# Step sizes' projection with both weight parts in one block of 128 columns, norms with shorter chains, one load per head

## The chip, the cores and the metric

The kernel runs on one core of one Trainium2 chip. The metric is device time in microseconds (us) of one execution, median of several. Engines are named as in the profile: PE (TensorE, matrix products), ACT (ScalarE), DVE (VectorE), POOL (GpSimd), SP (SyncE, which here only issues DMAs).

## What is computed

A trunk of two layers on 512 tokens of width 1024, all float32. Each layer is a token mixer and a GeGLU channel mixer, each between two RMS norms. The first mixer is retention and neighbourhood attention, the second a bidirectional state-space mixer (SSD). Cut to what the change touches:

```
def rms_norm(x, g):
    y = x * rsqrt(mean(x * x, axis=-1) + EPS)
    return y * g

def ssd_mixer(hn, w_in, ...):
    z, xbc, dt_raw = split(hn @ w_in)                # dt_raw: 64 step sizes per token
    dt = softplus(dt_raw + dt_bias)
    log_a = dt * -exp(a_log)                         # summed over the tokens of a chunk
    y = bidir_scan(q, k, x * dt_f, x * dt_b, log_a)  # per head: exp of differences of sums
    y = (y + x * d_skip) * silu(z)
    y = y * rsqrt(mean(y * y, over each of 4 groups) + EPS) * norm_g
    return y @ w_out

for layer in range(2):
    x = x + rms_norm(mixer(rms_norm(x, g0)), g1)
    x = x + rms_norm(ffn(rms_norm(x, g2)), g3)
```

## The kernel before

The 512 tokens are four tiles (t = 0 to 3) of 128 rows. Activations stand transposed on chip, features on partitions, as `xh` and `xl`: a float32 value is split into a rounded part (`hi`, written by an ACT copy) and the rest (`lo`, written by a DVE subtraction); `split`, L80 to L83, does that. Weights arrive as `wst` and are split in the same way into `whi` and `wlo`. A product is then three matmuls (`mm3`, L85 to L89): hi with hi, lo with hi, hi with lo; the product of both rests is left out.

Norms. `norm` squares a row tile on ACT with a running sum (`sumsq`, output thrown into a scratch tile `junk` of the ring `tmp`), DVE adds epsilon (`v_x`), POOL raises to the power -0.5 (`r_x`), and DVE scales into `xs` (L132). `turn` transposes `xs` on PE (`pt`, L141) and splits it into `xh`, `xl`. Behind a mixer, `post_half` squares each half row (`ssm0`, `ssm1`) and multiplies it by the gain (`mg`, L151); `post_norm` then adds the two sums (`v_m`, L110), POOL makes `r_m`, and DVE adds into `x` (L176).

The second mixer, `mixer1`, works through four groups of eight heads. `steps` projects the 64 step sizes (L589 to L598), makes softplus, prefix sums and their exponentials, and leaves them in two DRAM scratch tensors, `pd` (sums) and `yd` (decays), in `etot` (decay of a whole chunk, spread over the partitions by a matmul into `pe`, L635) and in `tok` (per-token factors: `lp_e`, whose logarithm is taken at L650, and `sw`, both transposed at L655). `load` brings one head's rows of `pd`, spread over 128 partitions, as `pb`; `head` adds `tok` (eight ACT pieces, L754), selects, and takes `e` (L758). `inter` and `pair` make the outputs `pi` and `py` of two heads each, `rms` the group norm (`pss`, one-column matmuls of squares with `mean`, then POOL's power `rg`). Weights of the next projections are used in between as fillers.

What sets the order: each group's list of slots (`SLOTS`) gives the program order, and a scheduler places every instruction on its engine's queue by its own estimates; engines run their queues strictly in that order. Tiles come from rings of fixed size, so a write also waits for the last reader of the memory it takes over. DMAs are issued by SP, those of `pb` by ACT.

The end of `mixer1` (the loop over `TAIL`) runs the output projection of the last group tile by tile, with the norms of the finished tiles between; the first matmuls of the channel mixer follow as soon as `xh` and `xl` of two tiles stand.

Of the kernel before, what the change touches and what calls it, by code (L numbers as in the profile page):

```python
# [10 lines left out]
U32 = mybir.dt.uint32  # L11
# [15 lines left out]
class Env:  # L27


    def __init__(self, ctx, tc):  # L30
# [11 lines left out]
        pool("pad", 1).tile([P, 32], F32, name="pad")  # L42
# [9 lines left out]
        self.x = self.res.tile([P, NT, D], F32, name="x")  # L52
# [53 lines left out]
    def inv_rms(self, name, a, b=None):  # L106
# [3 lines left out]
        nc.vector.tensor_scalar(v, a, EPS, b, op0=ALU.add, **({"op1": ALU.add} if b is not None else {}))  # L110
# [4 lines left out]
    def sumsq(self, src, n, name):  # L115

        s = self.small.tile([P, 1], F32, name=name)
        w = src.shape[-1]
        junk = self.tmp.tile([P, w], BF16, name="junk", tag="tmp")
        self.nc.scalar.activation(junk, src, AF.Square, scale=float(n) ** -0.5, accum_out=s)  # L120
# [14 lines left out]
    def turn(self, t):  # L135

        nc = self.nc
        for h, xs in enumerate(self.xs[t]):
# [15 lines left out]
    def finish(self, steps, st, done):  # L154
        for step in steps.split():
# [5 lines left out]
            elif t in self.xs:  # L161
                self.turn(t)
# [136 lines left out]
def mixer0(E, w0, w_v, w_fm, tabs, dist_d, logit, gn, bias, w_out, g_post_row, done):  # L299
# [254 lines left out]
def mixer1(E, w_dt, w_fm, cw, dtc, cols, mask, w_out, g_post_row, done):  # L554
# [7 lines left out]
    with ExitStack() as ctx:  # L562
# [25 lines left out]
        def steps():  # L588
# [479 lines left out]
```

## Time and profile before

| what | value |
|---|---|
| median of 3 runs | 1425.6 us (1424.62 to 1425.9) |
| the profiled execution | 1426.99 us |
| its span in the trace | 1425.2 us (1.8 us lie around it) |
| PE busy | 1398.7 us, 98% |
| DVE, ACT, POOL busy | 909.0, 706.9, 61.1 us |

PE has 26 us of idle time in all; whatever moves the time must remove PE work, remove such idle time, or change the clock at which PE runs. The trace gives PE's granted clock as a share of 2.4 GHz: 1.00, or 0.50, which is 1.2 GHz. Starts and lengths below are in us from the start of the span; a matmul's row shows its own latency, and matmuls of 512 columns follow each other at about 0.23 us.

### The profile page before, as it was taken

What the parts mean: (1) busy time and instruction counts of PE and PEld (TensorE: products, weight loads), DVE (VectorE), ACT (ScalarE), POOL (GpSimd) and SP (SyncE); (2) the same over time, 40 slices, a digit from 0 to 9 for tenths busy, and PEclk for the clock granted to TensorE, in tenths of its full rate; (3) what the DMA queues carried; (4) which work ended last, traced back from release to release, by engine and by line L of the source; (5) the groups of instructions that cost most, each with busy time, mean ns of one, the idle gap of its engine ahead of it and who ended that gap; (6) DMA issues with size and microseconds to landing.
All of it is one profiled execution on the core that took longest, in us unless ns stands there. A gap on an engine that the chain in (4) does not pass through costs nothing.

```text
span 1425.2 us, 17860 instructions
## 1 busy us (share of the span) xinstructions
PE 1398.7 (98%) x6838; PEld 1143.5 (80%) x6838; DVE 909.0 (64%) x1359; ACT 706.9 (50%) x1192; POOL 61.1 (4%) x66
## 2 busy tenths in 40 slices
PE   7999999999999999999999999999989999999998
PEld 6877776898888888888778788787878888888886
DVE  7378888666565652447788786897785665664232
ACT  5346666444444431334777888585354444443230
POOL 0010110100000000000000110000110000000000
PEclk9999999999999999999999999999999999999999
DMA  8443232233323223323556454463342233233231
GB/s 286 150 133 99 85 97 76 84 101 97 100 92 104 89 89 113 111 109 108 141 172 192 134 189 148 135 167 98 114 151 74 90 103 91 101 97 96 89 104 59
DMA packets 56949, 166.34 MB, mean 117 GB/s; under 512 B 7200, under 2 KB 7968, under 8 KB 56864
## 3 DMA queue, kind: packets, MB, share of 16 engines
q1 hardware_dynamic: 47648, 148.42, 32.4%
q10 hardware_dynamic: 9216, 16.78, 4.4%
q8 instruction: 54, 0.88, 0.2%
q14 instruction: 31, 0.25, 0.1%
HBM read 157.57 MB, written 5.51 MB: 114 GB/s over the span
## 4 chain that ended last, share of the span: by engine, by line
PE 91%; ACT 3%; DVE 3%; issue 1%; DMA 1%; POOL 0%; DVEq 0%; SPq 0%; POOLq 0%; ACTq 0%
PE mm L87 27%; PE mm L88 27%; PE mm L89 27%; PE pi L775 2%; PE st L723 1%; PE py L795 1%; PE y L450 1%; PE pt L141 1%; PE pt L667 1%; PE sc L434 1%; PE sc L435 0%; DMA x<-in_x 0%; PE pt L502 0%; PE y L512 0%; PE sc L485 0%
## 5 line engine op out<-in xcount | busy, mean ns | idle before, releaser
L87 PE MATMUL mm<-xh,whi 128*128 128x512 f32 (+1 forms) x1216 | 465.1, 383 | 2.5 <-ACT z L693 2.0
L89 PE MATMUL mm<-xl,whi 128*128 128x512 f32 (+2 forms) x1216 | 464.4, 382 | 3.0 <-DVE xl L83 3.0
L88 PE MATMUL mm<-xh,wlo 128*128 128x512 f32 (+2 forms) x1216 | 463.5, 381 | 0.0
L83 DVE TENSOR_TENSOR wlo<-wst,whi 128x1024 fp32r<-128x1024 f32 (+1 forms) x208 | 254.9, 1226 | 132.3 <-ACT whi L82 130.5
L82 ACT CAST whi<-wst 128x1024 fp32r<-128x1024 f32 (+1 forms) x208 | 216.6, 1043 | 151.4 <-PE mm L88 109.2
L87 PEld LDWEIGHTS mm<-xh,whi 128*128 128x128 f32 x1216 | 229.2, 188 | 48.3 <-issue 2.7
L89 PEld LDWEIGHTS mm<-xl,whi 128*128 128x128 f32 (+1 forms) x1216 | 229.1, 189 | 47.5 <-DVE xl L83 3.2
L88 PEld LDWEIGHTS mm<-xh,wlo 128*128 128x128 f32 (+1 forms) x1216 | 229.3, 189 | 42.5 <-issue 0.4
L228 DVE SCALAR_TENSOR_TENSOR cv<-mm,cwt,cv 128x511 f32<-128x511 f32 x88 | 66.0, 750 | 149.9 <-ACT cv L227 149.9
L227 ACT ACTIVATE cv<-mm,cwt 128x512 f32<-128x512 f32 x88 | 68.7, 780 | 127.6 <-PE mm L89 127.6
L87 PE MATMUL mm<-whi,hh 128*128 128x512 f32 x288 | 112.0, 389 | 0.0
L88 PE MATMUL mm<-whi,hl 128*128 128x512 f32 x288 | 112.0, 389 | 0.0
L89 PE MATMUL mm<-wlo,hh 128*128 128x512 f32 x288 | 112.0, 389 | 0.0
L754 ACT ACTIVATE pb<-pb,tok 128x128 f32<-128x128 f32 x256 | 79.6, 392 | 5.5 <-DMA pb<-pd 2.8
L82 ACT CAST hh<-cv 128x512 fp32r<-128x512 f32 x44 | 27.3, 621 | 103.4 <-DVE cv L236 103.4
L229 DVE SCALAR_TENSOR_TENSOR cv<-mm,cwt,cv 128x511 f32<-128x511 f32 x88 | 66.0, 750 | 3.0
L88 PEld LDWEIGHTS mm<-whi,hl 128*128 128x128 f32 x288 | 54.1, 188 | 11.3
L87 PEld LDWEIGHTS mm<-whi,hh 128*128 128x128 f32 x288 | 54.1, 188 | 11.2
L89 PEld LDWEIGHTS mm<-wlo,hh 128*128 128x128 f32 x288 | 54.1, 188 | 11.2
L687 DVE SCALAR_TENSOR_TENSOR xf<-mm,cwt,xf 128x511 f32<-128x511 f32 (+1 forms) x64 | 47.5, 744 | 8.5 <-ACT xf L684 8.1
L83 DVE TENSOR_TENSOR hl<-cv,hh 128x512 fp32r<-128x512 f32 x44 | 30.5, 693 | 28.9 <-ACT hh L82 28.9
L120 ACT ACTIVATE junk<-mm 128x512 bf16<-128x512 f32 x24 | 14.2, 594 | 66.0 <-PE mm L89 66.0
(249 smaller groups left out, 1873.3 us busy)
## 6 DMA issues: line engine op xcount, KB each, us to landing
wst<-in_f_up SPq DMA_DIRECT2D x88, 512.0 KB
wst<-in_f_down SPq DMA_DIRECT2D x44, 512.0 KB
wst<-in_c_fm SPq DMA_DIRECT2D x40, 512.0 KB
pb<-pd ACTq DMA_DIRECT2D x64, 256.0 KB
wst<-in_ab_fm SPq DMA_DIRECT2D x20, 512.0 KB
gain<-yd SPq DMA_DIRECT2D x32, 256.0 KB
wst<-in_c_out SPq DMA_DIRECT2D x16, 512.0 KB
gain<-in_norms SPq DMA_DIRECT2D x8, 512.0 KB
```

Of the source, the lines that this page charges most:

```text
L82: self.nc.scalar.copy(hi, src)
L83: self.nc.vector.tensor_tensor(lo, src, hi.bitcast(F32), op=ALU.subtract)
L87: mm(out, lh, rh, start=first, stop=False)
L88: mm(out, ll, rh, start=False, stop=False)
L89: mm(out, lh, rl, start=False, stop=last)
L141: nc.tensor.transpose(pt[:, j], xs[:, j * P:(j + 1) * P], self.ident)
L227: nc.scalar.activation(o, ps, AF.Identity, scale=w(1), bias=w(3))
L228: nc.vector.scalar_tensor_tensor(o[:, 1:], ps[:, :S - 1], w(0), o[:, 1:], op0=ALU.mult, op1=ALU.add)
L229: nc.vector.scalar_tensor_tensor(o[:, :S - 1], ps[:, 1:], w(2), o[:, :S - 1], op0=ALU.mult, op1=ALU.add)
L687: nc.vector.scalar_tensor_tensor(r[:, a], ps[:, b], wc(j), r[:, a], op0=ALU.mult, op1=ALU.add)
L754: nc.scalar.activation(pb[dr][:, c], pb[dr][:, c], AF.Identity, scale=1.0 - 2 * dr, bias=tok[:, 0, c, dr * H + h:dr * H + h + 1])
L775: nc.tensor.matmul(pi[:, c - 1 + dr], o["st"][dr, i][:, q * P:(q + 1) * P], o["t"][1][:, c * C:(c + 1) * C], start=True, stop=True)
```

## The change

In `steps` the two weight parts of a block of 128 features are put side by side as 128 columns, and each block is multiplied once by `xh` and once by `xl`: 16 matmuls with 128 rows of result instead of 24 with 64. The two halves of the result are added by DVE. In the norms, epsilon comes in as a 1025th column of `x` (so `v_x` is gone), `v_m` and `r_m` are made in `post_half` ahead of the second `mg`, and `junk` is one constant tile. Each head's `pb` is one DMA of 512 KB instead of two of 256 KB; the first three are issued by SP. The last group's `pss` is split in two: `q` sums the first three pairs' squares before the last pair. The last `turn` of a mixer gives its splits a higher priority.

```diff
-        self.x = self.res.tile([P, NT, D], F32, name="x")
+        xe = self.res.tile([P, NT, D + 32], F32, name="x")
+        nc.vector.memset(xe[:, :, D:D + 1], (EPS * D) ** 0.5)
+        self.x, self.xe = xe[:, :, :D], xe[:, :, :D + 1]
+        self.junk = self.const.tile([P, 1280], BF16, name="junk")
...
+    def power(self, name, v):
+        nc = self.nc
         r = self.small.tile([P, 1], F32, name="r_" + name)
         nc.gpsimd.tensor_tensor(r, v, self.mhalf, op=ALU.pow)
         return r
...
-        ss = self.sumsq(self.x[:, t, :], D, "ssx")
-        r = self.inv_rms("x", ss)
+        r = self.power("x", self.sumsq(self.xe[:, t, :], D, "ssx"))
...
-            self.split(self.xh[o], self.xl[o], pt)
+            with self.tc.high_priority(ahead) if ahead else nullcontext():
+                self.split(self.xh[o], self.xl[o], pt)
...
+        halves = st.setdefault(t, [])
+        r = self.inv_rms("m", halves[0][0], s) if halves else None
         (eng or nc.vector).tensor_tensor(m, ps, g_post[:, n * 512:(n + 1) * 512], op=ALU.mult)
-        st.setdefault(t, []).append((s, m))
+        halves.append((s, m, r))
...
-    "G h0 s0 s1 t9 h1 t8 s2 i0 t6 S h2 t7 p0 i1 S h3 o0 p1 i2 h4 h5 o1 p2 i3 h6 h7 p3",
+    "G h0 s0 s1 t9 h1 t8 s2 i0 t6 S h2 t7 p0 i1 S h3 o0 p1 i2 h4 h5 o1 p2 i3 h6 q h7 p3",
...
-            wh = E.whi.tile([P, 512], R32, name="whi")
-            wl = E.wlo.tile([P, 512], R32, name="wlo")
-            E.split(wh, wl, st)
+            w = E.whi.tile([P, KD, 2, H2], R32, name="whi")
+            E.split(w[:, :, 0], w[:, :, 1], st.rearrange("p (k h) -> p k h", k=KD))
             ps = E.mm.tile([P, S], F32, name="mm")
             for k in range(KD):
-                c = slice(k * H2, k * H2 + H2)
-                E.mm3(ps[:H2], wh[:, c], wl[:, c], E.xh[:, k], E.xl[:, k], k == 0, k == KD - 1)
+                for j, x in enumerate((E.xh, E.xl)):
+                    nc.tensor.matmul(ps, w[:, k].rearrange("p a h -> p (a h)"), x[:, k], start=k + j == 0, stop=k + j == KD)
...
                 nc.scalar.activation(z[i * H2:i * H2 + H2], ps[:H2, i * 256:i * 256 + 256], AF.Identity,
                                      bias=bc[:H2, 0:1])
+                nc.vector.tensor_tensor(z[i * H2:i * H2 + H2], ps[H2:, i * 256:i * 256 + 256], z[i * H2:i * H2 + H2], op=ALU.add)
...
-        def load():
+        def load(eng):
             if heads:
-                h = heads.pop(0)
-                pbs.append([three.tile([P, NT, C], F32, name="pb", bufs=6) for _ in range(2)])
-                for dr in range(2):
-                    nc.scalar.dma_start(pbs[-1][dr], pd[dr * H + h].partition_broadcast(P))
+                pbs.append(three.tile([P, 2, NT, C], F32, name="pb", bufs=3))
+                eng.dma_start(pbs[-1].rearrange("p r c l -> p r (c l)"),
+                              pd.rearrange("(r h) s -> h r s", r=2)[heads.pop(0)].partition_broadcast(P))
...
         for _ in range(3):
-            load()
+            load(nc.sync)
...
-            E.finish(TAIL[t], st, done)
+            E.finish(TAIL[t], st, done, 100 if t == NT - 1 else 0)
```

The scheduler places much of `mixer1` anew. The first place is PE's queue in the projections of the first group, where `steps` hands over its results; names are as above, and rows of `mm` are projections of the same group. Before:

```order
L635 MATMUL pe<-diag,ones 128x256
L655 MATMUL pt<-head,lp_e 128x128 x2
L88 MATMUL mm<-xh,wlo 128x512
L89 MATMUL mm<-xl,whi 128x512
L87 MATMUL mm<-xh,whi 128x512
L88 MATMUL mm<-xh,wlo 128x512
```

and in the changed kernel:

```order
L92 MATMUL mm<-xh,wlo 128x512
L93 MATMUL mm<-xl,whi 128x512
L91 MATMUL mm<-xh,whi 128x512
L92 MATMUL mm<-xh,wlo 128x512
L665 MATMUL pt<-head,lp_e 128x128 x2
L665 MATMUL pt<-head,sw 128x128 x2
L677 MATMUL pt<-head,bf 128x128 x4
L677 MATMUL pt<-head,xf 128x128 x16
L722 MATMUL pg<-cf,bf 128x128 x4
```

Between the last matmul of `steps` and `pe` stood 106 matmuls of 512 columns, and now stand 137. Between `pe` and the `lp_e` transposes stood none, and now stand 9.

The second place is ACT's queue at the same point, from `etot` to the first pieces of `pb`. Before:

```order
L637 COPY etot<-pe 128x2x2x64
L644 ACTIVATE sw<-tm 32x256
L656 COPY tok<-pt 128x2x2x64 x2
L693 ACT_TABLE_LOAD
L693 ACTIVATE xf<-xf 128x512
L744 DMA pb<-pd 128x512 x6
L668 COPY bt<-pt 128x512
L668 COPY xt<-pt 128x4x128 x2
L696 ACTIVATE xf<-xf 128x512
L754 ACTIVATE pb<-pb,tok 128x128 x3
```

and in the changed kernel, as far as the first `z`:

```order
L647 COPY etot<-pe 128x2x2x64
L654 ACTIVATE sw<-tm 32x256
L655 ACTIVATE sw<-pf 32x256
L660 ACT_TABLE_LOAD
L660 ACTIVATE lp_e<-lp_e 128x256
L86 CAST whi<-wst 128x1024
L666 COPY tok<-pt 128x2x2x64 x2
L678 COPY bt<-pt 128x512
L678 COPY xt<-pt 128x4x128 x4
L724 COPY gt<-pg 128x512
L763 ACTIVATE pb<-pb,tok 128x128 x4
L736 COPY state_5648<-st 128x512
```

The logarithm of `lp_e` now stands behind `etot`; it stood far ahead of it. The two `whi` that stood between the last piece of `pb` and `e` are gone from there, so what follows the pieces is a table load, `e`, a table load and `z`.

The third place is DVE's queue in the tail of `mixer1`, from the scaling of tile 1 (`xs`) to the split of a weight of the channel mixer (`wlo`). Before:

```order
L132 SCALAR_TENSOR_TENSOR xs<-x,r_x,gain 128x512 x2
L151 TENSOR_TENSOR mg<-m,gain 128x512
L851 SCALAR_TENSOR_TENSOR m<-mm,rg,x 128x512
L110 TENSOR_SCALAR v_m<-ssm_8899,ssm_8920 128x1
L151 TENSOR_TENSOR mg<-m,gain 128x512
L176 SCALAR_TENSOR_TENSOR x<-mg,r_m,x 128x512 x2
L83 TENSOR_TENSOR xl<-pt,xh 128x4x128 x2
L110 TENSOR_SCALAR v_x<-ssx 128x1
L83 TENSOR_TENSOR wlo<-wst,whi 128x1024
```

and in the changed kernel:

```order
L139 SCALAR_TENSOR_TENSOR xs<-x,r_x,gain 128x512 x2
L114 TENSOR_SCALAR v_m<-ssm_8770,ssm_8790 128x1
L869 SCALAR_TENSOR_TENSOR m<-mm,rg,x 128x512
L87 TENSOR_TENSOR xl<-pt,xh 128x4x128 x2
L185 SCALAR_TENSOR_TENSOR x<-mg,r_m,x 128x512 x2
L161 TENSOR_TENSOR mg<-m,gain 128x512
L869 SCALAR_TENSOR_TENSOR m<-mm,rg,x 128x512
L87 TENSOR_TENSOR wlo<-wst,whi 128x1024
```

`xl` of tile 1 now stands ahead of four operations that it stood behind; `wlo` stands behind the same operations as before, less the two small ones.

## Rows read from the trace of the kernel before

**Rows 1.** The page, the chain of work that ended last, shares by engine.

```profile
PE 91%; ACT 3%; DVE 3%; issue 1%; DMA 1%; POOL 0%; DVEq 0%; SPq 0%; POOLq 0%; ACTq 0%
```

**Rows 2.** Waits of PE: who for whom, us in total, times, longest.

```profile
PE pt L141 <- DVE xs L132: 9.7, 3, 7.3
PE mm L89 <- DVE xl L83: 3.0, 1, 3.0
PE mm L87 <- ACT z L693: 2.0, 1, 2.0
...
PE py L795 <- DVE e L760: 0.7, 1, 0.7
```

**Rows 3.** Windows, PE alone: window, length, PE busy, PEclk, DMA share, GB/s.

```profile
721.14:727.97 6.83, 6.12 (x31) 0.50 0.87 320
1031.75:1035.16 3.41, 3.41 (x10) 0.50 0.36 124
1055.64:1059.06 3.42, 3.42 (x18) 0.50 0.52 160
```

**Rows 4.** Groups by form, 654 to 670 us: busy, mean ns, idle before.

```profile
L88 PE MATMUL mm<-xh,wlo 128*64 128x512 f32 x8 | 3.1, 393 | 0.0
```

**Rows 5.** Timeline of PE, 689 to 697 us: start, us, instruction.

```profile
689.21 0.39 PE L87 MATMUL mm<-xh,whi 128*128 128x512 f32 x1
...
691.93 0.39 PE L87 MATMUL mm<-xh,whi 128*128 128x512 f32 x1
692.25 0.70 PE L635 MATMUL pe<-diag,ones 128*128 128x256 f32 x2
```

**Rows 6.** Timeline of ACT, 692 to 721 us.

```profile
693.65 0.63 ACT L637 COPY etot<-pe 128x256 f32<-128x256 f32 x1
...
696.06 1.28 ACT L693 ACT_TABLE_LOAD   x1
696.11 1.37 ACTq L744 DMA_DIRECT2D pb<-pd  x3
...
704.10 0.99 ACT L754 ACTIVATE pb<-pb,tok 128x128 f32<-128x128 f32 x3
...
709.68 4.21 ACT L754 ACTIVATE pb<-pb,tok 128x128 f32<-128x128 f32 x14
713.79 1.99 ACT L82 CAST whi<-wst 128x1024 fp32r<-128x1024 f32 x2
...
719.04 0.60 ACT L693 ACTIVATE z<-mm 128x512 f32<-128x512 f32 x1
```

**Rows 7.** Tile lp_e: xcount, duration ns min/median/max, first and last start.

```profile
L650 ACT ACTIVATE lp_e<-lp_e x1: 418/418/418, 687.7 to 687.7; 128x256 f32<-128x256 f32 x1
L651 DVE SCALAR_TENSOR_TENSOR lp_e<-pf,bc,lp_e x1: 481/481/481, 692.1 to 692.1; 128x256 f32<-128x256 f32 x1
```

**Rows 8.** Timeline of PE, 1028 us, and of all engines, 1046 to 1063 us.

```profile
1028.45 1.92 PE L824 MATMUL pss<-mean,sq 128*128 128x1 f32 x16
...
1049.39 1.29 PE L141 MATMUL pt<-head,xs 128*128 128x128 f32 x8 [1.15 <-DVE xs L132]
...
1052.33 1.41 DVE L176 SCALAR_TENSOR_TENSOR x<-mg,r_m,x 128x512 f32<-128x512 f32 x2 [0.43 <-POOL r_m L112]
...
1055.10 1.21 DVE L83 TENSOR_TENSOR wlo<-wst,whi 128x1024 fp32r<-128x1024 f32 x1
...
1056.37 0.33 SPq L62 DMA_DIRECT2D wst<-in_f_up  x1
...
1059.97 1.05 ACT L82 CAST whi<-wst 128x1024 fp32r<-128x1024 f32 x1 [3.75 <-DMA wst<-in_f_up]
...
1062.63 0.39 PE L87 MATMUL mm<-xh,hh 128*128 128x256 f32 x1 [0.20 <-ACT hh L82]
```

**Rows 9.** Timeline, the last 6 us of the span.

```profile
1419.27 0.69 DVE L151 TENSOR_TENSOR mg<-mm,gain 128x512 f32<-128x512 f32 x1 [5.27 <-ACT junk L120]
1419.88 0.21 DVE L110 TENSOR_SCALAR v_m<-ssm,ssm 128x1 f32<-128x1 f32 x1
```

More of the change, by code (lines that the diff above doesn't have):

```diff
@@ L1 @@
-from contextlib import ExitStack
+from contextlib import ExitStack, nullcontext
 import concourse.bass as bass
@@ L41, in __init__ @@
         self.small = pool("small", 6)
-        pool("pad", 1).tile([P, 32], F32, name="pad")
+        pool("pad", 1).tile([P, 80], F32, name="pad")
         self.mm = pool("mm", 4, space=PSUM)
@@ L104, in proj_fm, with inv_rms @@
                      self.xh[:, k, c0:c1], self.xl[:, k, c0:c1], k == 0, k == KD - 1)
[L106 removed]
+    def inv_rms(self, name, a, b):
         nc = self.nc
         v = self.small.tile([P, 1], F32, name="v_" + name)
[L110 removed]
+        nc.vector.tensor_scalar(v, a, EPS, b, op0=ALU.add, op1=ALU.add)
+        return self.power(name, v)
+    def power(self, name, v):
+        nc = self.nc
         r = self.small.tile([P, 1], F32, name="r_" + name)
@@ L118, in sumsq @@
         w = src.shape[-1]
-        junk = self.tmp.tile([P, w], BF16, name="junk", tag="tmp")
-        self.nc.scalar.activation(junk, src, AF.Square, scale=float(n) ** -0.5, accum_out=s)
+        self.nc.scalar.activation(self.junk[:, :w], src, AF.Square, scale=float(n) ** -0.5, accum_out=s)
         return s
@@ L133, in norm, with turn @@
             self.xs[t].append(xs)
-    def turn(self, t):
+    def turn(self, t, ahead=0):
         nc = self.nc
@@ L150, in post_half, with finish @@
             m = self.tmp.tile([P, 512], F32, name="mg", tag="tmp")
+        halves = st.setdefault(t, [])
+        r = self.inv_rms("m", halves[0][0], s) if halves else None
         (eng or nc.vector).tensor_tensor(m, ps, g_post[:, n * 512:(n + 1) * 512], op=ALU.mult)
-        st.setdefault(t, []).append((s, m))
-    def finish(self, steps, st, done):
+        halves.append((s, m, r))
+    def finish(self, steps, st, done, ahead=0):
         for step in steps.split():
@@ L161, in finish @@
             elif t in self.xs:
-                self.turn(t)
+                self.turn(t, ahead)
     def flush(self):
@@ L753, in head @@
                 for c in range(NT):
-                    nc.scalar.activation(pb[dr][:, c], pb[dr][:, c], AF.Identity, scale=1.0 - 2 * dr,
+                    nc.scalar.activation(pb[:, dr, c], pb[:, dr, c], AF.Identity, scale=1.0 - 2 * dr,
                                          bias=tok[:, 0, c, dr * H + h:dr * H + h + 1])
-            nc.vector.copy_predicated(pb[1], um.bitcast(U32).rearrange("p (o l) -> p o l", o=1).broadcast_to([P, NT, C]), pb[0])
+            nc.vector.copy_predicated(pb[:, 1], um.bitcast(U32).rearrange("p (o l) -> p o l", o=1).broadcast_to([P, NT, C]), pb[:, 0])
             e = three.tile([P, NT, C], F32, name="e")
-            nc.scalar.activation(e, pb[1], AF.Exp)
-            load()
+            nc.scalar.activation(e, pb[:, 1], AF.Exp)
+            load(nc.scalar)
             o["m"][j] = e, nc.vector.tensor_tensor(e, e, o["gt"], op=ALU.mult)
@@ L817, in pair, with squares, part @@
             o["y"].append((yh, yl))
-        def rms(o):
-            pss = E.px.tile([P, NT], F32, name="pss", tag="px")
-            for c in range(NT):
-                for i, sq in enumerate(o["sq"]):
-                    E.together([nc.tensor.matmul(pss[:, c:c + 1], sq[:, c * C:(c + 1) * C], mean, start=i == 0,
-                                                 stop=sq is o["sq"][-1])], o["sqw"][2:])
-            ss = few.tile([P, NT], F32, name="ss", bufs=2)
-            nc.vector.tensor_scalar(ss, pss, EPS, None, op0=ALU.add)
+        def squares(o, sq, waits):
+            pss = E.px.tile([P, NT], F32, name="pss", tag="px")
+            E.together([nc.tensor.matmul(pss[:, c:c + 1], sq[:, c * C:(c + 1) * C], mean, start=True, stop=True)
+                        for c in range(NT)], waits)
+            return pss
+        def part(o):
+            o["ss"] = few.tile([P, NT], F32, name="ss", bufs=2)
+            nc.vector.tensor_scalar(o["ss"], squares(o, o["sq"][0], o["sqw"][2:]), EPS, None, op0=ALU.add)
+        def rms(o):
+            if "ss" in o:
+                nc.vector.tensor_tensor(o["ss"], squares(o, o["sq"][1], o["sqw"][3:]), o["ss"], op=ALU.add)
+            else:
+                part(o)
             o["r"] = few.tile([P, NT], F32, name="rg", bufs=2)
-            nc.gpsimd.tensor_tensor(o["r"], ss, E.mhalf.broadcast_to([P, NT]), op=ALU.pow)
+            nc.gpsimd.tensor_tensor(o["r"], o["ss"], E.mhalf.broadcast_to([P, NT]), op=ALU.pow)
         def out_mm(o, t, ws):
@@ L877, in mixer1 @@
         for _ in range(3):
-            load()
+            load(nc.sync)
         tiles(gs[0], 3)
@@ L899, in mixer1 @@
                     rms(o)
+                elif a == "q":
+                    part(o)
                 elif a == "t":
```

5 lines of the change are left out of this document (2 added, 3 removed).

## Prediction

> **What bounds the kernel now.** I read the chain of work that ended last first: PE holds 91% of it [rows 1], so the time is PE's work, PE's waits and PE's clock. The list of PE's waits comes next. It shows four of some size: 9.7 us for transposes of `xs`, 7.3 of them at the start of the program, 3.0 for `xl` in the tail of the second mixer, 2.0 for `z` and 0.7 for `py` [rows 2]. Then the clock: three stretches in mid-program ran at 0.50, which is 1.2 GHz, of 6.83, 3.41 and 3.42 us [rows 3]. Work done there takes twice as long, so they cost at most 3.4, 1.7 and 1.7 us. The first begins 1.5 us after the wait for `z` ends at 719.64 [rows 6]. The second follows a stretch of 1.92 us in which PE ran sixteen one-column matmuls of `pss`, and the third follows the wait for `xl`; the wait of 1.15 us before the transposes at 1049.39 was followed by none until then [rows 8]. So a wait here costs more than its length when it is 2 us or longer.
>
> The Trainium skill (TensorE: Matmul & The Clock Gate, section HAM oscillation) says that a matmul stream which keeps waiting for its data runs cold after each wait. The trace agrees for the two long waits and goes further with the `pss` stretch, where PE was not idle. By that rule the new wait in the tail, below, would be followed by half clock; the sum takes the same from rows.
>
> **The projection of the step sizes.** 24 matmuls become 16. One takes 0.393 us of latency with 64 columns of weights [rows 4] and 0.39 with 128 [rows 5], so the wider block costs nothing. Matmuls follow each other at 0.227: twelve intervals lie between 689.21 and 691.93 [rows 5]. Saved: 8 x 0.227 = 1.8 us of PE. The two additions of the halves (64x256) are not in the trace. The nearest row, a DVE operation on 128x256, took 0.48 [rows 7], so 0 to 1.0 us are added to the chain that leads to `pe`. What covers them are the matmuls between `steps` and `pe`, now 137 instead of 106; I take nothing.
>
> **Where the saved 1.8 us go.** PE's content from `steps` to the first matmul that needs `z` is otherwise the same, only its order changes. `pe` began at 692.25 [rows 5]; now it comes 31 matmuls later and 1.8 earlier: 692.25 + 7.0 - 1.8 = 697.45, done after 0.70 at 698.15. ACT, which waits for it, then runs `etot` (0.63), two `sw` (256 columns each, taken as 0.42 like the logarithm), a table load (1.28) and the logarithm (0.42), and DVE adds 0.48 [rows 6, 7]: 698.15 + 0.63 + 0.84 + 1.28 + 0.42 + 0.48 = 701.8. PE meanwhile has nine matmuls, 2.0 us, and stands at the `lp_e` transposes from 700.1. That is a new wait of 1.7 us, bounded by 0 (if the logarithm's table is there) and 2.7 (if the additions come late). It eats the saving: PE reaches the first matmul behind `z` when it did, at 719.64 - 2.0 = 717.6 [rows 2, 6]. Behind the waiting transposes stand those of `sw`, `bf` and `xf`, and behind them ACT's copies.
>
> **When `z` comes.** It ended at 719.04 + 0.60 = 719.64, behind 24 pieces of `pb`, the last at 713.79, and two `whi` of together 1.99 [rows 6]. Now the two `whi` are not there; from the last piece on, 719.64 - 713.79 - 1.99 = 3.9 us remain. The pieces depend on the first `pb`. Its DMA, now on SP, takes over memory that the `sw` transposes read last, so it is issued at about 702.6, against 696.11 before. Behind it in SP's queue stand the other two `pb` and the `gain` loads for `inter`. How long 512 KB take I bound by a weight load of 512 KB, 1056.37 to 1059.97, 3.6 us [rows 8], and by the first `pb` before, which was used at 704.10, 8.0 after its issue [rows 6]. The load is alone in front of its queue, so I take a value near the first: 4.1, landing at 706.7. ACT is through with its copies by about 706.5. Then 24 pieces at 4.21 / 14 = 0.30 [rows 6] and two copies of state at 0.6 (as `etot`) make 8.4: last piece 715.1, `z` at 719.0. **Term: -0.6** (bounds -1.0 and +3.3).
>
> PE's wait for `z` is then 719.0 - 717.6 = 1.4 us instead of 2.0. Between `z` and `py` stand 18 matmuls instead of 10, 4.1 us, and the second `e`, which `py` waited for, moves with `z`; that wait goes: **-0.7**. The clock: where one wait of 2.0 stood there are now one of 1.7 and one of 1.4, 16 us apart. The 1.4 lies nearer to the 1.15 that no drop followed than to the 2.0. A drop after the first wait would only use up the second. So I take the stretch at 721.14 as gone: **-3.4** (bounds 0 and -3.4).
>
> **Norms.** `v_x` goes from each chain, and `v_m` with `r_m` runs beside the second `mg`. At the end of the program `v_m` started 0.61 after `mg` [rows 9] and will start where `mg` did: **-0.6** (bounds 0 and -0.7). At the start one small DVE operation (0.21 as `v_m`) leaves the chain of the second tile, while the first waits for its gain: **-0.2** (0 to -0.5). The other norms lie beside matmuls of the channel mixers.
>
> **The tail of the second mixer.** `xl` of tile 1 now comes ahead of the four operations that held it; the 3.0 us go. What is late next is a weight. Its load is issued when `wlo` is done (1055.10 + 1.21; issue at 1056.37), lands 3.6 later, and behind `whi` and the `hh` copies PE's next matmuls start at 1062.63 [rows 8]. `wlo` still stands behind the same DVE operations; it gains only the two small ones (0.1 each) and most of the 0.43 wait for `r_m` [rows 8]: 0.5. So PE arrives about 4 us early and waits until 1062.1. The stretch at 1055.64 cost nothing before, since PE had only 0.20 left to wait at 1062.63; a drop after the new wait lies in dense matmuls and costs 1.7, the price of 3.4 us at half clock [rows 3]. **Term: -0.5 + 1.7 = +1.2** (bounds -1.4, if no drop follows and the one after `pss`, now two stretches of half the length, goes as well, and +2.9 for two such stretches). One DMA for each head and the fixed `junk` take issues off ACT, which has time over; nothing.
>
> **Sum.** -0.6 - 0.7 - 3.4 - 0.6 - 0.2 + 1.2 = -4.3. From the profiled 1426.99 that is 1422.7. The profiled execution stands 1.4 over the median of 1425.6, so on the median's scale: **1421.3**.
>
> **Rivals.** *The half clock stays* behind the wait for `z`. For it: 1.4 and 1.7 are both more than the 1.15 that passed. Without the -3.4 the sum is -0.9, 1424.7; with `z` no earlier than before -0.3, 1425.3. In this case the change does not do what it says: 1.8 us less work on PE, and all of it stands in a wait.
>
> *The tail keeps its full clock*, or PE is through with the drop while it still waits. For it: a wait of 4 us can hold much of a stretch of 3.4. Then the 1.7 goes and the time is 1419.6, and 1418.7 if the second stretch goes too, since an `m` waits in it.
>
> *The first `pb` lands late*, slower than before. All of ACT stands behind its first piece: both state copies, 24 pieces, `e`, `z`. For it: SP shares the engines with the `gain` loads, and the old loads took up to 8.0. At 8.0 it lands at 710.6, `z` comes at 710.6 + 8.4 + 3.9 = 722.9, 3.3 later than before, the half clock stays, and the sum is +3.3 - 0.7 - 0.6 - 0.2 + 1.2 = +3.0, 1428.6. That is the point from which it decides; each us more costs a us. Against it: the load is first in its queue.
>
> **How the numbers follow.** A measurement here can tell about 0.2%, 2.85 us, from no change. Chances: the forecast 0.40, the half clock stays 0.37, the tail keeps its clock 0.17, a late `pb` 0.06. Faster by over 0.2% (under 1422.75) are the first and third: 0.57; same 0.37; slower 0.06. The range reaches from 1418.2, the third rival with the lower bounds of `z`, to 1425.4; the forecast's own is 1420.0 to 1422.7.
>
> **What would show it.** Right: PE waits of 1 to 2.5 us at the `lp_e` transposes and of 1 to 2 at `z`; no wait for `py`; full clock from 715 to 730; no wait for `xl`, but one of 3 to 4.5 for `hh`, with half clock behind it; `r_m` beside `mg` at the end. Wrong: a `pb` that lands after 708, a stretch of half clock behind `z`, a wait of PE that stands in none of these places, or `wlo` over 1 us earlier against PE's matmuls.

## The result and the profile after

The changed kernel takes 1429.55 us in the median (17 runs, 1427.54 to 1431.77), the kernel before 1425.60 beside it (17 runs). The ratio is 1.0023, with a 95% interval of 1.0016 to 1.0031: slower by some 0.2%, where 1421.3 and faster was forecast. The profiled execution took 1427.88 us and lies at the fast end of its runs, that of before 1.4 above its median. So the two traces stand only 0.9 us apart. What the traces show explains that 0.9 in full; the rest of the 3.3 to 4 us is looked for below.

From the page, the first section: PE's busy time fell by 3.0 us and its span still grew.

```profile
span 1426.0 us, 17815 instructions
...
PE 1395.7 (98%) x6830; PEld 1142.6 (80%) x6830; DVE 909.7 (64%) x1347; ACT 710.1 (50%) x1193; POOL 61.6 (4%) x66
```

The waits of PE, in the changed kernel (us in total, times, longest), answer to [rows 2]:

```profile
PE pt L148 <- DVE xs L139: 8.9, 3, 8.4
PE mm L91 <- ACT hh L86: 3.8, 2, 3.1
PE mm L91 <- ACT z L703: 3.5, 1, 3.5
PE pt L665 <- DVE lp_e L661: 2.5, 1, 2.5
```

`xl` and `py` are gone from the list, as forecast. `lp_e` is new at 2.5 (1.7 forecast), `hh` is new at 3.1 (some 4 forecast), and `z` went from 2.0 up to 3.5 where 1.4 was forecast.

Windows, PE alone, answer to [rows 3] (window, length, PE busy, PEclk, DMA share, GB/s):

```profile
703.90:707.40 3.50, 3.50 (x20) 0.53 0.34 101
724.60:727.90 3.30, 3.30 (x10) 0.50 0.65 198
1031.00:1034.50 3.50, 3.50 (x21) 1.00 0.04 14
1062.30:1065.60 3.30, 2.94 (x12) 0.53 0.59 166
```

One stretch of half clock stands behind each of the three new or longer waits; behind `pss`, now in two pieces of about 1 us, there is none (nor is there one in b_steps and b_loads below, which have it in one piece). PE's timeline around the first two:

```profile
703.29 0.44 PE L665 MATMUL pt<-head,lp_e 128*128 128x128 f32 x2 [2.52 <-DVE lp_e L661]
...
704.32 3.47 PE L677 MATMUL pt<-head,xf 128*128 128x128 f32 x16
...
723.87 0.50 PE L91 MATMUL mm<-xh,whi 128*128 128x512 f32 x1 [3.54 <-ACT z L703]
```

ACT's timeline over the same time answers to [rows 6]:

```profile
695.52 1.28 ACT L652 ACT_TABLE_LOAD   x1
...
699.52 0.61 ACT L647 COPY etot<-pe 128x256 f32<-128x256 f32 x1
...
701.00 1.28 ACT L660 ACT_TABLE_LOAD   x1
...
706.27 0.59 ACT L678 COPY xt<-pt 128x512 f32<-128x512 f32 x1 [0.27 <-PE pt L677]
...
708.72 0.59 ACT L724 COPY gt<-pg 128x512 f32<-128x512 f32 x1 [0.31 <-PE pg L722]
709.20 1.28 ACT L763 ACTIVATE pb<-pb,tok 128x128 f32<-128x128 f32 x4
...
714.67 4.87 ACT L763 ACTIVATE pb<-pb,tok 128x128 f32<-128x128 f32 x16 [1.99 <-DMA pb<-pd]
...
723.22 0.60 ACT L703 ACTIVATE z<-mm 128x512 f32<-128x512 f32 x1
```

The copies behind the transposes wait 0.27 for each, while PE transposes at half clock. The first `pb` piece comes at 709.20, and then the second head's load makes ACT stand for 1.99. 16 pieces, `e` and two table loads follow, and only then `z`.

To place the time, I cut both spans at the same instructions: the start of the last transpose of `xs` ahead of `steps` (653.39 before, 654.10 after), the first `st` of the second group (795.2 and 797.2), the last matmul (1418.06 and 1419.50) and the end.

| part | before | after | difference | forecast |
|---|---|---|---|---|
| start to the last turn ahead of `steps` | 653.39 | 654.10 | +0.7 | -0.2 |
| from there to the second group's first `st` ("the stretch") | 141.8 | 143.1 | +1.3 | -4.7 |
| to the last matmul, with the tail of `mixer1` | 622.8 | 622.3 | -0.5 | +1.2 |
| to the end | 7.1 | 6.55 | -0.6 | -0.6 |

The stretch closes on the rows. Before it lost 2.0 + 0.7 in waits and half of 6.12 to 6.83 to the clock, 5.8 to 6.1 [rows 2, 3]. Now it loses 2.5 + 3.5 in waits and half of 3.5 + 3.3, 9.4, and PE has 1.8 less to do: that makes +1.5 to +1.8 (9.4 - 1.8, less the 5.8 to 6.1), against +1.3 measured.

### The profile page after: what moved, and what is told of

Read it like the earlier page. It is cut to its first block, busy times and chain, and to the rows that moved or that the text cites. A ratio compares the mean times of both kernels' runs of the same rounds, so it can differ in the third digit from the quotient of the medians.

```text
span 1426.0 us, 17815 instructions
## 1 busy us (share of the span) xinstructions
PE 1395.7 (98%) x6830; PEld 1142.6 (80%) x6830; DVE 909.7 (64%) x1347; ACT 710.1 (50%) x1193; POOL 61.6 (4%) x66
## 4 chain that ended last, share of the span: by engine, by line
PE 87%; DVE 6%; ACT 3%; issue 2%; DMA 1%; POOL 1%; SPq 0%; DVEq 0%; POOLq 0%; ACTq 0%
PE mm L91 26%; PE mm L92 26%; PE mm L93 26%; PE pi L784 1%; PE py L804 1%; PE st L733 1%; DVE wlo L87 1%; PE y L459 1%; DVE xf L697 1%; DMA pb<-pd 1%; PE pt L148 1%; PE sc L443 1%; PE pt L677 0%; PE sc L444 0%; DMA x<-in_x 0%
## 5 line engine op out<-in xcount | busy, mean ns | idle before, releaser
L93 PE MATMUL mm<-xl,whi 128*128 128x512 f32 (+1 forms) x1208 | 461.5, 382 | 0.0
L92 PE MATMUL mm<-xh,wlo 128*128 128x512 f32 (+1 forms) x1208 | 459.4, 380 | 0.0
L87 DVE TENSOR_TENSOR wlo<-wst,whi 128x1024 fp32r<-128x1024 f32 x207 | 254.5, 1230 | 133.2 <-ACT whi L86 131.4
L93 PEld LDWEIGHTS mm<-xl,whi 128*128 128x128 f32 x1208 | 227.4, 188 | 43.8 <-issue 1.4
L92 PEld LDWEIGHTS mm<-xh,wlo 128*128 128x128 f32 x1208 | 227.7, 188 | 41.9 <-issue 0.2
```

The costliest lines, as they stand in the source:

```text
L87: self.nc.vector.tensor_tensor(lo, src, hi.bitcast(F32), op=ALU.subtract)
L92: mm(out, ll, rh, start=False, stop=False)
L93: mm(out, lh, rl, start=False, stop=last)
```

## The experiments

Fifteen kernels ran. Ratios are against the kernel before, run beside each, with the 95% interval. "Stretch" is the part of that name above, in the profiled execution; the waits and the clock are those inside it. A trace is one execution and need not lie at the median: that of b_loads took 1425.14 us, with half clock at 91 us, far ahead of the stretch.

| kernel | median us | ratio | stretch | waits of PE over 1 us | half clock |
|---|---|---|---|---|---|
| before | 1425.60 | | 141.8 | `z` 2.0 | 721 to 728 |
| changed | 1429.55 | 1.0023 [1.0016, 1.0031] | 143.1 | `lp_e` 2.5, `z` 3.5 | 704 to 707.5, 724.5 to 728 |
| a_nosteps | 1422.06 | 0.9969 [0.9958, 0.9980] | 136.8 | none | none |
| a_noloads | 1424.94 | 0.9988 [0.9979, 0.9997] | 140.1 | `lp_e` 2.5 | 702 to 706 |
| a_nonorms | 1428.44 | 1.0018 [1.0008, 1.0028] | 144.3 | `lp_e` 2.5, `z` 4.3 | 722.5 to 729.5 |
| a_table | 1429.42 | 1.0019 [1.0010, 1.0028] | 143.9 | `z` 4.0, `lp_e` 2.5 | 722.5 to 729.5 |
| b_steps | 1423.29 | 0.9986 [0.9977, 0.9995] | 140.3 | `lp_e` 2.5 | 703 to 707 |
| b_loads | 1420.80 | 0.9971 [0.9962, 0.9980] | 137.9 | `pi` 1.1 | none |
| b_normsq | 1426.52 | 0.9999 [0.9989, 1.0008] | 139.9 | `z` 2.0, `py` 1.6 | none |
| f_lnearly | 1424.83 | 0.9993 [0.9984, 1.0001] | 141.5 | `py` 3.1 | 719 to 726.5 |
| x_add | 1427.33 | 1.0014 [1.0003, 1.0025] | 141.5 | `py` 2.4 | 722 to 726 |
| y_noadd | 1429.61 | 1.0024 [1.0012, 1.0036] | 145.1 | `sw` 2.2, `py` 1.3, `whi` 2.6 | 735.5 to 743 |
| a_actload | 1425.56 | 0.9999 [0.9990, 1.0009] | 139.3 | `lp_e` 2.5, `z` 1.3 | none |
| f_lnact | 1431.91 | 1.0039 [1.0026, 1.0052] | 148.3 | `z` 2.2, `whi` 5.6 | 718.5 to 722.5, 739 to 746.5 |
| f_zfirst | 1425.11 | 0.9992 [0.9981, 1.0003] | 140.1 | `lp_e` 2.5 | 703 to 707 |
| f_zln | 1430.20 | 1.0029 [1.0016, 1.0041] | 143.8 | `z` 5.1 | 721 to 728.5 |
| f_zln4 | 1422.89 | 0.9979 [0.9970, 0.9988] | 137.4 | none | none |

### Parts taken away, one at a time

**a_nosteps**: the changed kernel with the projection of before.

```diff
-                for j, x in enumerate((E.xh, E.xl)):
-                    nc.tensor.matmul(ps, w[:, k].rearrange("p a h -> p (a h)"), x[:, k], ...)
+                E.mm3(ps[:H2], wh[:, c], wl[:, c], E.xh[:, k], E.xl[:, k], k == 0, k == KD - 1)
...
-                nc.vector.tensor_tensor(z[i * H2:i * H2 + H2], ps[H2:, ...], z[i * H2:i * H2 + H2], op=ALU.add)
```

> The changed kernel with the old projection of the step sizes (24 matmuls with 64 columns of weights, no addition of halves); everything else as changed. Theory A (the loss in the second mixer comes from the new order that the new projection brings: pe behind 31 more matmuls, the logarithm of lp_e behind etot, so a wait of 2.5 us at the lp_e transposes with half clock behind it, and late pb): no wait at lp_e over 0.3, PE reaches the matmul behind z about 1 us later than it could but z comes by 720; 3 to 4 us faster than the changed kernel, ratio to the kernel before 0.9995 to 1.0003. Theory B (the single loads on SP land late, whatever the projection): the wait for z stays over 2.5 us and the ratio stays at 1.0015 to 1.003.

Both waits and both stretches of half clock go, the stretch shortens by 6.3 us, and the time is 0.31% under the kernel before. With 1.8 us more work on PE it is 7.5 us faster than the changed kernel, about twice what theory A allowed; theory B is refuted.

**a_noloads**: the changed kernel with two loads for each head, all issued by ACT, as before.

```diff
-                pbs.append(three.tile([P, 2, NT, C], F32, name="pb", bufs=3))
-                eng.dma_start(pbs[-1]..., pd.rearrange("(r h) s -> h r s", r=2)[heads.pop(0)]...)
+                for dr in range(2):
+                    nc.scalar.dma_start(pbs[-1][dr], pd[dr * H + h].partition_broadcast(P))
```

> The changed kernel with two loads of 256 KB for each head, all issued by ACT, as before; the rest as changed. Theory A: the lp_e wait of 2.5 us and the half clock behind it stay, and z moves ahead of most pieces of pb in ACT's order, so the wait for z shrinks, but e and py come late instead; ratio 1.001 to 1.0025. Theory B: the loss goes with the loads, ratio 0.9985 to 1.000.

The `lp_e` wait and its half clock stay, `z` is waited for 0.8 us. So far that is theory A; but `py` is not waited for in its place, and the ratio lies in the range of theory B. Here the scheduler puts `z` on ACT behind 8 pieces of `pb` and not behind 24 and `e`.

**a_nonorms**: the changed kernel with the norms and priorities of before.

```diff
...
-        r = self.power("x", self.sumsq(self.xe[:, t, :], D, "ssx"))
+        ss = self.sumsq(self.x[:, t, :], D, "ssx")
+        r = self.inv_rms("x", ss)
...
```

> The changed kernel with the norms of before (epsilon by DVE, v_m behind mg, junk in the ring, no higher priority of the last splits); projection, loads and split pss as changed. Theory A: the first transposes come at 7.3 instead of 8.4, which gives back 0.7 us, the end of the program takes 0.6 more, and the wait for xl in the tail returns; ratio 1.002 to 1.003, as the changed kernel within noise. A third theory (the norms as a whole cost, by ACT's first table load): ratio at most 1.0015.

No difference that can be measured from the changed kernel: the new projection and the loads alone are enough for the loss. This trace also shows something that the changed kernel's hides. Up to `lp_e` it runs within 0.1 us of it, and the wait there is the same, but no half clock follows. ACT is then through with its copies 1.7 us earlier, at 707.6, and it doesn't help:

```profile
704.83 2.06 ACT L669 COPY xt<-pt 128x512 f32<-128x512 f32 x4
706.99 0.59 ACT L715 COPY gt<-pg 128x512 f32<-128x512 f32 x1
708.99 1.28 ACT L754 ACTIVATE pb<-pb,tok 128x128 f32<-128x128 f32 x4 [1.41 <-DMA pb<-pd]
...
714.58 2.45 ACT L754 ACTIVATE pb<-pb,tok 128x128 f32<-128x128 f32 x8 [2.19 <-DMA pb<-pd]
...
723.41 0.60 ACT L694 ACTIVATE z<-mm 128x512 f32<-128x512 f32 x1
```

ACT waits for the first load, issued at 703.91, until 709.0, and for the second until 714.6. `z` comes when it came in the changed kernel (723.22), and PE, not held up by the clock, waits longer for it: 4.3.

**a_table**: the changed kernel with a one-column square at the start, which brings ACT's first table in early.

```diff
+        nc.scalar.activation(self.junk[:, 1279:], self.mhalf, AF.Square)
```

> The changed kernel with one ACT activation of a single column ahead of all others, so that its table is loaded before x arrives. First transposes at about 7.1 to 7.3 instead of 8.41 by the theory that the first square's table load waits for x because the square has two waits now; 0.7 to 1.1 us faster than the changed kernel, ratio 1.0015 to 1.002. By the rival (x itself lands later) the first transposes stay at 8.4.

It tests the +0.7 of the start. In the kernel before, the first table load began at 0.73. In the changed one it waits for the load of `x`. The likely reason, which no run isolates, is that the square behind it now waits for two things, that load and the column of epsilon:

```profile
4.49 1.28 ACT L128 ACT_TABLE_LOAD   x1 [4.49 <-DMA x<-in_x]
```

With the early load the first transposes begin at 7.21 instead of 8.41. The ratio lies in the expected range, but it can't be told from the changed kernel's, and 0.19% are lost all the same: the 1.1 us at the start are not what made the kernel slower. In the traces they don't even reach `steps`: a_table comes to the last turn at 654.46 and a_nonorms, which begins at 7.42, at 654.04. Ten other kernels with the new start come there between 653.0 and 655.3, and b_normsq, with half clock at 92 us, at 657.8. So the +0.7 of the table is no more than what one execution differs from another by.

### Parts alone

**b_steps**, **b_loads** and **b_normsq** are the kernel before with one part of the diff above: the projection, the loads, and the norms with priorities and the split `pss`.

```diff
+                for j, x in enumerate((E.xh, E.xl)):
+                    nc.tensor.matmul(ps, w[:, k].rearrange("p a h -> p (a h)"), x[:, k], ...)
```

> The kernel before with the new projection alone (16 matmuls and the two additions). Theory C (what decides is when the chain of small DVE operations behind the projection ends; the new projection ends it 6 us later, and this costs little while ACT issues the loads, because z stands ahead of most pieces of pb in that order): lp_e wait near 2.5 us, z wait under 1.5, ratio 0.998 to 1.000. Theory D (the projection is worth its eight matmuls and the loads alone do the harm): no wait at lp_e, ratio 0.9985 or less.

```diff
+                pbs.append(three.tile([P, 2, NT, C], F32, name="pb", bufs=3))
...
+            load(nc.sync)
```

> The kernel before with one load per head alone, the first three issued by SP. Theory C: pe stays at about 692, pb is loaded earlier than before, z by 717, no half clock between 715 and 730; py about 4 to 5 us earlier; ratio 0.996 to 0.998. Theory B (the loads on SP land late by themselves): ratio over 1.000.

```diff
+        r = self.inv_rms("m", halves[0][0], s) if halves else None
...
+    "G h0 s0 s1 t9 h1 t8 s2 i0 t6 S h2 t7 p0 i1 S h3 o0 p1 i2 h4 h5 o1 p2 i3 h6 q h7 p3",
```

> The kernel before with the norms, the higher priority and the split pss alone. By the step of the forecast (end -0.6, start now +0.4 to +0.7 by the table load that waits for x, tail -0.5 to -2 by the trace of the changed kernel): ratio 0.9983 to 1.0000. By the forecast as it stood (tail +1.2): 1.0003 to 1.001.

Alone they bring -0.14%, -0.29% and -0.01%. The sum would be -0.44%, and together they give +0.23%: two parts that are good alone spoil each other. In b_loads `z` stands behind all 24 pieces too, but the first piece begins 49.0 us after the last turn; in the changed kernel 55.1 us after it. `z` ends at 723.64 there, later than expected, but the first `py` stands ahead of what needs it on PE, and PE doesn't wait for `z`. The ratio of b_normsq lies in the first of the two ranges named for it, and its interval reaches into the second, so it doesn't tell how large the term of the tail is.

### What the new projection delays

**x_add** has the 24 matmuls of before, and on DVE two operations in the place of the additions. A maximum with the projection stands in the place of the sum, so what it computes is not the same.

```diff
-                nc.vector.tensor_tensor(z[...], ps[H2:, i * 256:i * 256 + 256], z[...], op=ALU.add)
+                nc.vector.tensor_tensor(z[...], ps[:H2, i * 256:i * 256 + 256], z[...], op=ALU.max)
```

> The changed kernel with the old 24 matmuls, and with two DVE operations of 64x256 added where the halves would be added (a maximum with the projection itself, so the step sizes become wrong). Theory C: the two operations alone, with no matmul saved, move pe to 698 to 700 and bring the loss back; ratio 1.0005 to 1.0025, against 0.9969 without them. Theory D: they cost what they take, under 1 us; ratio 0.997 to 0.9978.

**y_noadd** has the 16 matmuls and no additions; the product with the rests of the weights is left out of the step sizes.

```diff
-                nc.vector.tensor_tensor(z[...], ps[H2:, i * 256:i * 256 + 256], z[...], op=ALU.add)
```

> The changed kernel with the 16 matmuls but without the two additions of the halves (the part of the weights' rest is left out of the step sizes). Theory C: the saved matmuls alone are worth up to 1.8 us against the old projection, less what waits for z; the chain of small operations ends 2 to 3 us earlier than in the changed kernel, the logarithm stands ahead of etot, pb and z are early: ratio 0.996 to 0.998, near the 0.9969 without the projection. Rival F (fewer matmuls ahead of the chain do the harm by themselves): ratio over 0.9995.

From the last turn, `pe` begins after 38.9 us before, 44.0 in the changed kernel, 44.0 in x_add and 41.0 in y_noadd. So two more DVE operations bring the whole delay of `pe` with the old matmuls too, and without them 2.1 of the 5.1 us remain. The loss of x_add shows at `py` (2.4), not at `lp_e` and `z`: its logarithm still stands ahead of `etot`. DVE's timeline of the changed kernel shows how `pe` comes late: the two additions are 0.43 us each, but what follows them is a chain of some 20 small operations, and DVE's queue weaves other work into it.

```profile
669.24 0.43 DVE L618 TENSOR_TENSOR z<-mm,z 64x256 f32<-64x256 f32 x1
...
670.84 0.42 DVE L277 SCALAR_TENSOR_TENSOR lp_e<-z 128x256 f32<-128x256 f32 x1
...
693.92 0.69 DVE L629 TENSOR_TENSOR_SCAN pf<-msk,la 128x256 f32<-128x256 f32 x1
```

The first operation of the chain comes 1.5 us later than before (669.31), the scan 6.0 (687.91): the chain takes 4.5 us longer, since three more `xf` operations of 0.74 and three more `wlo` of 1.22 stand in it.

y_noadd was to be faster than before if the delay of `pe` were all, and was the miss of this group: its ratio is that of rival F. But b_steps has the 16 matmuls too and gains, so fewer matmuls alone are not what costs. ACT changes tables once more for `sw` there, and further on PE waits for a weight cast that ACT's queue holds behind pieces of `pb` and `e`:

```profile
700.13 0.44 PE L664 MATMUL pt<-head,sw 128*128 128x128 f32 x2 [2.19 <-DVE sw L656]
...
735.65 0.74 PE L91 MATMUL mm<-xh,whi 128*128 128x512 f32 x1 [2.63 <-ACT whi L86]
```

An early `pe` is not enough: here the order of ACT's queue is what comes late.

### What makes `z` late

**a_actload**: single loads, issued by ACT.

```diff
-            load(nc.sync)
+            load(nc.scalar)
```

> The changed kernel with all single loads issued by ACT, none by SP; z then stands behind 8 pieces of pb in ACT's queue, not 24. Theory C (the place of z behind 24 pieces of late pb is the loss): lp_e wait 2.5 us as before, z wait under 1.5, ratio 0.998 to 0.9995, as with two loads per head. Theory B (one load of 512 KB lands later than two of 256 KB): ratio over 1.001.

The three loads are issued at 705.29 to 706.71, later than in the changed kernel (703.97 to 705.39), and the first piece begins at 713.52 and not 709.20; still `z` is waited for 1.3 us and not 3.5, with 4.0 us less in the median (the ratio is 0.0004 above the range of theory C, within its interval). So an earlier load is not what `z` needs. ACT's timeline shows the reason: `z` stands behind 8 pieces.

```profile
716.23 0.70 ACT L763 ACTIVATE pb<-pb,tok 128x128 f32<-128x128 f32 x2
716.95 1.28 ACT L703 ACT_TABLE_LOAD   x1
718.24 0.60 ACT L703 ACTIVATE z<-mm 128x512 f32<-128x512 f32 x1
```

**f_lnearly**: the logarithm of `lp_e` written ahead of the prefix sums.

```diff
+                ex = lpp.tile([P, 256], F32, name="lp_e")
+                nc.vector.tensor_scalar(ex, dt, 1e-20, None, op0=ALU.max)
+                nc.scalar.activation(ex, ex, AF.Ln)
...
-                nc.scalar.activation(ex, ex, AF.Ln)
```

> The changed kernel with the logarithm of lp_e and its clamp written ahead of the prefix sums, so that it stands ahead of etot on ACT again. Theory C: the wait of 2.5 us at the lp_e transposes goes, but z does not come earlier by more than 2 us since the chain and the loads of pb end as late; the wait for z takes over most of it; ratio 1.000 to 1.002. Rival E (the place of the logarithm is the whole loss): ratio 0.997 to 0.9985, as without the new projection.

The `lp_e` wait goes and the kernel gains 0.3%, but a wait of 3.1 for `py` and 7 us of half clock take the place. The ratio lies between the two ranges, and it is not `z` that comes late next. **f_lnact** has that and the loads on ACT, and was expected to be the best of those with the new projection.

```diff
+                nc.scalar.activation(ex, ex, AF.Ln)
...
-            load(nc.sync)
+            load(nc.scalar)
```

> The changed kernel with both edits: logarithm written ahead of the prefix sums, and loads issued by ACT. Theory C: no wait at lp_e, z behind 18 pieces, waits of 1 to 2 us at z or py; ratio 0.997 to 0.9990, the best of those with the new projection. Rival: the two edits do not add, ratio 0.999 to 1.0005.

It is the slowest of all, outside both ranges. As in y_noadd, a weight cast comes late:

```profile
739.75 0.79 PE L91 MATMUL mm<-xh,whi 128*128 128x512 f32 x1 [5.59 <-ACT whi L86]
```

### `z` by itself

**f_zfirst**: the changed kernel, with the pieces of the second and third head held behind `z` on ACT.

```diff
+            o["lead"] = lead.ins
...
+            with tc.issue_after(o["lead"]) if h in (1, 2) else nullcontext():
```

> The changed kernel, with the pieces of pb of the second and third head written to follow the activation of z; PE's order up to the first py is the same but for projections moved ahead of py, and ACT's order is the same but that z stands behind 8 pieces and e instead of behind 24. Theory (z's place in ACT's queue behind pieces that come late is what costs): ACT reaches z by 716, so z waits only for the last matmul of z, and PE waits 0.6 to 1.2 us instead of 3.5, as in the kernels where z stands behind 8 pieces; no half clock at 724 to 728. That gives back 2.7 + 1.7 us: 1424.5 to 1426.0, ratio 0.9993 to 1.0003. The lp_e wait of 2.5 and its half clock stay. Rival 1 (the time is lost again downstream: e of the second and third head comes later, and py or a weight cast on ACT is waited for instead): a wait of 2 us or more at py or at a cast within 15 us of z, with half clock, and a ratio of 1.0015 to 1.003. Rival 2 (single placement does not matter, the loss is spread over the program): z's wait goes and the ratio stays at 1.0015 to 1.003 with no new wait.

ACT in f_zfirst:

```profile
711.36 0.99 ACT L765 ACTIVATE pb<-pb,tok 128x128 f32<-128x128 f32 x3
...
716.70 0.64 ACT L769 ACTIVATE e<-pb 128x512 f32<-128x512 f32 x1 [3.06 <-DVE pb L767]
...
720.05 0.60 ACT L703 ACTIVATE z<-mm 128x512 f32<-128x512 f32 x1 [0.98 <-PE mm L93]
```

Now ACT waits for the matmul of `z`, not PE for ACT: PE's wait is 0.7, the half clock behind it is gone, and the median falls by 4.4, from 1429.55 to 1425.11; 2.7 + 1.7 was expected. PE's work and its order up to here are those of the changed kernel, so the place of `z` on ACT is shown to cost this.

**f_zln**: the early logarithm with it.

```diff
+                nc.scalar.activation(ex, ex, AF.Ln)
...
+            with tc.issue_after(o["lead"]) if h in (1, 2) else nullcontext():
```

> The kernel with the logarithm written early, and z ahead of the pieces of the second and third head as well. Theory (steps and loads lose to each other only through these two places, lp_e and ACT's queue ahead of z and py): no wait at lp_e, z at most 1.2 us, no half clock from 695 to 735, and what the parts gave alone comes together: 0.14 + 0.29 per cent, 1419.5 to 1422.5, ratio 0.996 to 0.998. Rival (some other operation on ACT becomes the late one each time the order moves): a wait of over 2 us at py or at a weight cast, with half clock behind it, and a ratio of 0.9985 to 1.001, no better than the early logarithm alone (0.9993).

A miss, by the edit: three pieces of the fourth head now stood ahead of `z`, whose load was issued by ACT behind `e`, at 714.09. ACT in f_zln:

```profile
720.36 0.98 ACT L765 ACTIVATE pb<-pb,tok 128x128 f32<-128x128 f32 x3 [6.31 <-DMA pb<-pd]
721.36 1.28 ACT L703 ACT_TABLE_LOAD   x1
722.66 0.60 ACT L703 ACTIVATE z<-mm 128x512 f32<-128x512 f32 x1
```

**f_zln4** holds those pieces back too (the lines are against f_zln).

```diff
-            with tc.issue_after(o["lead"]) if h in (1, 2) else nullcontext():
+            with tc.issue_after(o["lead"]) if h in (1, 2, 3, 4) else nullcontext():
```

> As the kernel with both edits before it, but the pieces of the fourth head's pb are held behind z too: there three of them stood ahead of z, waited 6.3 us for their load (issued behind e at 714.1) and made z 5.1 us late. PE's order and all else is the same. Theory: ACT reaches z by 716 and z waits for its last matmul alone; no wait over 1.2 us and no half clock from 695 to 735; 5.1 - 0.7 + 3.4 = 7.8 us less than that kernel's 1.0029, a ratio of 0.9965 to 0.9985. Rival (an operation on ACT becomes the late one each time the order moves): a wait of over 2 us at py or at a weight cast by 750, with half clock behind it, and 0.9985 to 1.001.

The waits of PE in f_zln4:

```profile
PE mm L91 <- ACT z L703: 0.7, 1, 0.7
...
PE pt L665 <- DVE sw L660: 0.5, 1, 0.5
```

No wait over 0.7 in the stretch, no half clock, 0.9979: inside the range of the theory. The whole change with two orders mended beats the kernel before by 0.2%. It doesn't beat a_nosteps or b_loads (0.9969 and 0.9971; the intervals overlap), although PE has 1.8 us less to do. In its stretch PE waits four times, 0.46 to 0.69 and 2.25 in all, where a_nosteps has no wait over 0.3: that is where the saving went.

## Why the prediction was wrong

**When `z` comes** is the step that failed. It had the first load land at 706.7, 4.1 us after its issue, the pieces run from there without a gap, and `z` end at 719.0. The changed kernel comes to this place 0.7 late, so that makes 707.4 and 719.7. The first piece could start at 709.0 (a_nonorms, where ACT stood ready for it), 1.6 later, 5.1 after the issue. Then ACT stood 1.99 for the second load, which landed some 10 us after its issue; and `z` ended at 723.82. 1.6 + 2.0 and half a microsecond in ACT's own operations are the 4.1 that the term of -0.6 was off: measured it is +3.5. The loads of three heads and four `gain` were in flight together, with a DMA share of 0.53 from 705 to 708 and of 1.06 from 711 to 718; that this is what made them late is argued, not shown. The sum took the first head's load as the only one that matters.

**The half clock** behind the first new wait "would only use up the second": right, as a_nonorms shows, where without that drop PE waits 4.3 for `z` and not 3.5. But the term of -3.4 rested on a wait for `z` of 1.4. With 3.5 the drop behind it stays, and with that at `lp_e` there are again 6.8 us of half clock. The wait for `py` (-0.7) did go. The drop at `lp_e` is hidden in the wait for `z`, so of the -3.4 the trace shows some -1.4: 3.06 were lost before (half of 6.12), and 1.7 are now. In the forecast's own terms the stretch is then +3.5 - 0.7 - 1.4 = +1.4 and not -4.7; +1.3 was measured.

**The additions** were priced at nothing, with 137 matmuls as their cover. Their duration was right, 0.43 each. The price is that of the new order behind them, 4.5 us in a chain of small operations (x_add, y_noadd). The forecast took `pe`'s place from the order and so had its time right (697.45, measured 698.11 less 0.7), and `lp_e` nearly (1.7 forecast, 2.5 measured, bound 2.7), but did not ask why it was late or what else would be.

**The rival on the other side**, a first `pb` that lands late, is what came, and its 1428.6 is near the 1429.55 measured. It was given 0.06 because the load is first in its queue. It decided from a landing at 710.6 (711.3 with the 0.7); the landing at 709.0 did it together with the second load, which no rival had. That its number is near is in part luck: its stretch was +2.6, twice what the trace shows.

**The tail** is -0.5 between the two traces where +1.2 was forecast, but that says more of the one trace of before than of the change. Its half clock behind `pss` [rows 3, 8] is missing in b_steps and b_loads, whose `pss` is that of before. In b_steps (the second line is a window: length, PE busy, PEclk, DMA share, GB/s):

```profile
1026.01 1.84 PE L825 MATMUL pss<-mean,sq 128*128 128x1 f32 x16
...
1027.85:1039.26 11.41, 11.34 (x49) 1.00 0.48 160
```

From the start of `pss` to the first transposes of the tail these two take 13.25 and 13.26 us, and before 14.65. So sixteen one-column matmuls need not be followed by half clock, as the forecast read it, and it is not shown that the split of `pss` took it away. From the second group's first `st` to the last matmul b_steps and b_loads take 621.4 and 621.5 us, and the thirteen kernels with the new norms 621.9 to 623.3. Against these two the part got longer by 0.4 to 1.9, and +1.2 is not refuted.

The pieces of the term can be read from the changed kernel:

```profile
1047.19 1.28 DVE L87 TENSOR_TENSOR xl<-pt,xh 128x512 fp32r<-128x512 f32 x2
...
1049.48 1.29 PE L148 MATMUL pt<-head,xs 128*128 128x128 f32 x8 [0.26 <-DVE xs L139]
...
1054.62 1.22 DVE L87 TENSOR_TENSOR wlo<-wst,whi 128x1024 fp32r<-128x1024 f32 x1
...
1061.56 0.38 PE L91 MATMUL mm<-xh,hh 128*128 128x256 f32 x1 [3.10 <-ACT hh L86]
```

PE arrives at the second transposes of the tail at 1048.24 before (1049.39 - 1.15) and at 1049.22 now. From there to the second product with `hh`, the last to be waited for (1062.63 and 1062.60), it takes 14.4 before and 13.4 now: -1.0, where -0.5 was forecast. `wlo` starts 1.5 earlier against PE, not 0.5, for DVE is 0.9 further already at these transposes. From there to the last matmul it takes 355.4 and 356.9: the half clock behind the wait for `hh` costs 1.5, where 1.7 was forecast.

**The end** was right, -0.6: `v_m` now starts ahead of the second `mg`, against [rows 9].

```profile
1420.71 0.21 DVE L114 TENSOR_SCALAR v_m<-ssm,ssm 128x1 f32<-128x1 f32 x1 [5.82 <-ACT junk L128]
1420.84 0.68 DVE L161 TENSOR_TENSOR mg<-mm,gain 128x512 f32<-128x512 f32 x1
```

**What stays open.** The traces of before and after differ by 0.9 us, the medians by 4.0. Of the 3 us between, the trace of before stands 1.4 above its median, as much as it loses behind `pss` (14.65 less 13.25). In a_nonorms and a_table, with the same two waits, the half clock lies otherwise and the stretch is 0.8 to 1.2 longer than in the changed kernel. In eight of the thirteen traces with the new norms the half clock at `hh` lasts 6.8 us and not 3.4, and the way from the second transposes of the tail to the last matmul is 370.6 to 371.5 long, against 370.3 in the changed kernel. Other executions of the changed kernel may be like these, which would make the rest, but no second trace of either kernel was taken. Why the scheduler places `z` behind 8 pieces in one kernel and behind 24 in another was not tried.

## What to carry to other kernels

Two changes that each help can lose together when the first makes a chain later and the second puts a needed operation behind the results of that chain in an in-order queue: look, on each engine, what stands behind the late operation, and move that first. When a cheap operation goes into a chain of small ones, read the new order of the engine that carries the chain; the operation's duration says little. Where several loads are issued together, price the one that the last needed piece waits for, not the first.

## What was not expected of the hardware

A wait of about 2 us is followed by half clock in some executions and not in others. The wait of 2.0 for `z` was, in the kernel before [rows 2, 3]; in b_normsq one of 2.0 at the same place was not, nor that of 2.2 for `sw` in y_noadd, while 2.2 for `z` in f_lnact was. All waits of 2.4 us or more inside the stretch were followed by one, except that of 2.5 for `lp_e` in a_actload, a_nonorms and a_table, which the changed kernel has as well, with the drop. Of the shorter ones, 0.5 to 1.6, none was. So the length of a wait alone doesn't settle it, and the forecast's comparison of 1.4 with 1.15 and 2.0 could not have. Nor do one-column matmuls: sixteen `pss` in a row were followed by half clock in the kernel before, and not in b_steps and b_loads.

The Trainium skill (TensorE: Matmul & The Clock Gate, section HAM oscillation) has a kernel whose stream runs cold after each wait for data of some 3 to 5 us. The runs agree: each wait of 3.0 to 5.6 us inside the stretch and in the tail was followed by half clock. The waits of 2.0 to 2.5 us that half clock followed are not among those it tells of.

A load of ACT's table took 1.28 us wherever it stood, and an activation that waited for nothing else began 0.02 us behind it (701.00 + 1.28, then 702.30).
